# Second attention branch's scores: two products of 128 rows and two of 64 rows per head instead of four of 128

## The chip, the cores and the metric

The kernel runs on one core of one Trainium2 chip. The metric is the device time of one execution in microseconds, the median of the runs shown. TensorE (PE) multiplies; VectorE (DVE), ScalarE (ACT) and GpSimd (POOL) do the elementwise work; the SyncE queue (SP) issues most DMAs. "PEld" is the loading of a product's stationary operand into TensorE's array.

## The reference: what is computed

One layer of a diffusion backbone: 1024 latent tokens of width 1024 and 256 context tokens. The hidden states are modulated, projected to queries, keys, values and gates, and go through two attention branches of 8 heads of 64 with 2 key heads each. Branch A is windowed, with a sink; branch B, the second, is global: every token attends to all 1024 latent and all 256 context keys.

```python
def _gqa_scores(q, k):
    return jnp.einsum("bqhgd,bkhd->bhgqk", q, k).astype(jnp.float32) * (HEAD_DIM ** -0.5)
...
def _global_attention(q, k_all, v_all):
    def one_block(i):
        q_blk = lax.dynamic_slice_in_dim(q, i * BLOCK, BLOCK, axis=1)
        p = jax.nn.softmax(_gqa_scores(q_blk, k_all), axis=-1)
        return _gqa_values(p, v_all)
```

Then gates, an output projection, a residual LayerNorm, a convolutional feed-forward of width 2816 and a second LayerNorm.

## The kernel before

**Numbers in two parts.** Every float32 operand of a product is split into a high part, rounded to the format that TensorE takes, and a low part, the remainder. A general product is three passes (mm3, lines 375 to 378): high by high, high by low, low by high. For the scores the contraction is only 64 long, so both parts fit into the 128 rows of the array together.

**The scores before.** Per head, `q1` is the transposed query tile with the high part in rows 0 to 63 and the low part in rows 64 to 127, and `q2` the same with the halves swapped. The keys `KL` (1024 latent, one tile per key head) and `KC` (256 context) hold [high; low] in the same way. `qk` (line 757) makes two passes over all 128 rows: q1 by the keys gives high·high and low·low, q2 gives low·high and high·low. For branch B, `scores` (line 769) calls it for two banks of 512 keys, so four products of 128 rows by 512 columns per head; `cscores` (line 804) does the 256 context keys of a unit's four heads, eight products of 256 columns.

**Units.** The attention is cut into 32 units: 16 of branch A, then 16 of branch B, each with one tile of 128 queries and one key head, so four query heads. A unit's queries are split on POOL (`qsplit`), turned by four transposes on PE (`qturn`, line 736), copied out by ACT into `q1` (`qcopy`, line 741) and swapped into `q2` by two DMAs of 64 rows on SP (`qswap`, line 745, its two issues at lines 747 and 748). Then come the context scores (sx), the four heads' scores (s), the maximum on DVE (line 793), the exponential on ACT (line 802), transposes of the probabilities on PE (pt, line 847), their split into hi and lo on ACT, DVE and POOL, and the products with the values (av, line 856). Groups of the first output projection (ptb, lines 376 to 378) fill in between.

**The order.** In the attention stage all engines are under a manual schedule. `graph` (line 154) makes one entry per step with its engine, cost and a key; `plan` (line 86) is a list scheduler that takes on each engine the ready step with the smallest key. COST, KEY, FILL and SLACK are tables of numbers that only set this order; every engine then executes its list strictly in it. `qdm` is the step of the swap, `scx` that of the context scores, `sc1` that of one head's scores in branch B.

**The keys' preparation.** `kv_post` (line 667) runs ten times, for eight tiles of latent keys and two of context keys. Its last split (line 697) puts the high part of all four key heads (heads 0 and 1 of branch A, 2 and 3 of branch B) into columns 0 to 63 of `ks` and the low part into columns 64 to 127; transposes on PE turn them into rows, and ACT copies them to `KL` and `KC`.

Of the kernel before, what the change touches and what calls it, by code (L numbers as in the profile page):

```python
# [7 lines left out]
F32 = mybir.dt.float32  # L8
# [5 lines left out]
P = 128  # L14
# [4 lines left out]
NT = 8  # L19
HD = 64  # L20
# [19 lines left out]
PWB = 5  # L40
DAH = 3
SINK = 640
POOLED, FILL, SUMS = ((0,), (1, 6)), (16.988136, 27.931), ('ot1', 'ot1')
LOOK, SLACK = 24, (0, 0, 0, 0, 0)
D3AT = (7, 5), (7, 9), (4, 1), (4, 4), (4, 7), (4, 10), (5, 2)
NXS = 5
RAWB = 3
# [18 lines left out]
PE, ACT, DVE, POOL, SP = range(5)  # L66
# [19 lines left out]
def plan(ops, rings, free, look, slack):  # L86
# [5 lines left out]
    while any(todo):  # L92
# [25 lines left out]
        for b in o.uses:  # L118
# [6 lines left out]


COST = dict(
    qhi=(POOL, .38, .49), qlo=(POOL, .71, .825), qtr=(PE, .28, .55), qcp=(ACT, .47, .675), qdm=(SP, 1.1, 2.9),
    sc0=(PE, .70, .945), sc1=(PE, .91, 1.16), scx=(PE, .94, 1.19),
    pm0=(DVE, .80, .97), pm1=(DVE, 1.26, 1.43), pmx=(DVE, .40, .56),  # L130
    ex0=(ACT, .83, .98), ex1=(ACT, 1.14, 1.30), exx=(ACT, .49, .65),
    nr0=(DVE, .18, .28), nr1=(DVE, .34, .44), st=(PE, .11, .36), rc=(ACT, .20, .34), dn=(SP, .30, 2.2),
# [1 line left out]
    tr=(PE, .436, .685), hi=(ACT, .47, .675), lo=(DVE, .605, .765), cp=(ACT, .47, .675), ph=(POOL, .59, .70),  # L134
# [9 lines left out]
PRING = "pt", "s", "av"  # L144
RINGS = dict(pt=3, s=2, av=1, qs=1, q1=2, q2=2, p=8, hi=4, lo=4, ptr=2, up=1, ot=1, rb=2, wraw=1, wh=1, wl=1)

KEY = {'qh': -0.919337, 'qt': -1.197497, 'sc': -0.139853, 'scs': (0.199825, 0.270357),
           'scx': -3.142963, 'tr': 0.868828, 'tru': (0.216182, 0.070723),
           'av': 1.348883, 'st': 1.265771, 'out': 0.885708, 'exd': 1.273589, 'st1': 1.664154, 'wb': (27.969376, 29.459582),
           'wg': (31.81419, 33.291489, 33.170198, 33.528645), 'ge': -0.046198, 'gr': 4.26668}  # L150
UNITS = 32


def graph(x, key=KEY, pooled=((3,), (2, 6)), fill=None, ot=("ot0", "ot1")):
    ops, last = [], {}
    def op(kind, k, fn, after=(), takes=(), uses=()):
        e, occ, lat = COST[kind]
        o = Op(e, kind, occ, lat, k, fn, after, takes, uses, kind in PORT)
        ops.append(o)
        return o  # L160
# [10 lines left out]
    for hf in (0, 1):  # L171
# [6 lines left out]
        for c in range(4):  # L178
            r = op("gr", key["gr"] + .6 * (4 * hf + c), lambda hf=hf, c=c: x.gr(hf, c), [e], uses=[tile])
        op("gd", key["gr"] + .6 * (4 * hf + c), lambda hf=hf: x.gd(hf), [r], uses=[tile])  # L180
    units = []
    for u in range(UNITS):
        br, i, g = u // 16, u % 16 // 2, u % 2
# [7 lines left out]
        U = float(u)  # L191
        q1, q2 = Buf("q1"), Buf("q2")
        if u >= 2:
            qs, pt = Buf("qs"), Buf("pt")
            a = op("qhi", U + key["qh"], lambda u=u, b=qs: x.qhi(u, b), takes=[qs])
            b_ = op("qlo", U + key["qh"], lambda u=u, b=qs: x.qlo(u, b), [a], uses=[qs])
            qlo = b_
            c = op("qtr", U + key["qt"], lambda u=u, b=qs, p=pt: x.qtr(u, b, p), [b_], [pt], [qs])
            chain("qtr", c)
            d = op("qcp", U + key["qt"], lambda u=u, q=q1, p=pt: x.qcp(u, q, p), [c], [q1], [pt])  # L200
            qr = op("qdm", U + key["qt"], lambda u=u, q=q1, r=q2: x.qdm(u, q, r), [d], [q2], [q1])
        else:
            qlo, qr = None, op("qdm", U - 9, lambda: None, takes=[q1, q2])
            qr.occ = qr.lat = 0.0
# [4 lines left out]
        if br:  # L209
            s, pc = Buf("s"), Buf("p")  # L210
# [8 lines left out]
        for h in range(4):  # L219
            k = U + key["sc"] + key["scs"][br] * h  # L220
            s = Buf("pt" if nar and h < 2 else "s")
# [31 lines left out]
        t = op("st", kn, lambda u=u, p=pt: x.st(u, p), [n_], [pt])  # L253
        r = op("rc", kn, lambda u=u, p=pt, b=rb: x.rc(u, p, b), [t], [rb], [pt])
# [3 lines left out]
        av = Buf("av")  # L258
        avo, trs = [], []
        for j, n in enumerate(kt):  # L260
            k = U + key["tr"] + j * key["tru"][br]
            ka = U + key["av"] + j * key["tru"][br]
            pt, hi, lo = Buf("pt"), Buf("hi"), Buf("lo")
# [6 lines left out]
            if j in pooled[br]:  # L270
                rw = Buf("ptr")
                c = op("cp", k, lambda u=u, n=n, p=pt, r=rw: x.cp(u, n, p, r), [o], [rw], [pt])
# [19 lines left out]
        c = op(ot[br], ko - .4, lambda u=u, o=o_: x.ot(u, o), [b_], [o_], [rw, up])  # L292
# [8 lines left out]
    for f2 in range(4):  # L301
# [4 lines left out]
        c = op("wl", k - .9, lambda f2=f2, r=raw, l=wl: x.wl(f2, r, l), [b_], [wl], [raw])  # L306
# [15 lines left out]
    for f2 in (0, 1):  # L322
# [4 lines left out]
        c = op("wl", k + .1, lambda f2=f2, r=raw: x.wl(4 + f2, r, None), [b_], uses=[raw])  # L327
# [26 lines left out]
def layer_kernel(  # L354
# [6 lines left out]
    nc = tc.nc  # L361
# [4 lines left out]
    def split(src, hi, lo, hi_eng, lo_eng):  # L366
        if hi_eng is nc.scalar:
            cast[:] = [nc.scalar.copy(hi, src).ins]  # L368
        elif hi_eng is nc.gpsimd:
            nc.gpsimd.tensor_scalar(out=hi, in0=src, scalar1=1.0, scalar2=0.0, op0=ALU.mult, op1=ALU.add)  # L370
        else:
            hi_eng.tensor_copy(hi, src)
        low[:] = [lo_eng.tensor_tensor(out=lo, in0=src, in1=hi.bitcast(F32), op=ALU.subtract).ins]  # L373
# [88 lines left out]
    sc, scc = ht("sc"), ht("scc")  # L462
# [21 lines left out]
    st1 = {}  # L484
# [38 lines left out]
    for n in (0, 1):  # L523
        s = slice(n * HALF, (n + 1) * HALF)
# [11 lines left out]
    for k in range(KT):  # L536
# [5 lines left out]
        for t in range(NT):  # L542
            s = slice(t * P, (t + 1) * P)
# [114 lines left out]
    KL, KC, VT = [], [], []  # L658
# [8 lines left out]
    def kv_post(t, acc):  # L667
        st = {}

        def s1():  # L670
            kv = st["kv"] = ph1.tile([P, 512], F32, tag="kv", name=f"kv{t}", bufs=KVB)
            nc.vector.tensor_tensor(out=kv, in0=acc, in1=bias_kv, op=ALU.add)
            kb = st["kb"] = kv[:, 128:256].rearrange("p (h d) -> p h d", d=HD)
            vt = VT[t // 2][:, t % 2]
            v3 = kv[:, 256:512].rearrange("p (h d) -> p h d", d=HD)
            nc.scalar.copy(vt[:, :, 0:HD], v3)
            tp = pw(f"ktp{t}")
            st["tp"] = tp = [tp[:, n * P:(n + 1) * P] for n in range(4)]
            st["ss"] = rms_scale(kb, 2, f"k{t}", tp[3])
            if t < NT:  # L680
                st["tb"] = ph1.tile([P, 2, HD], F32, tag="tb", name=f"tbk{t}", bufs=4)
                gfold(st["tb"], 1, t, nc.vector)
                rope(nc.vector, kv[:, 0:128], kv[:, 0:128], 2, ropec[:, t], ropes[:, t], f"ka{t}", tp[0], tp[1])
            nc.gpsimd.tensor_tensor(out=vt[:, :, HD:P], in0=v3, in1=vt[:, :, 0:HD].bitcast(F32), op=ALU.subtract)

        def s2():
            kv, kb = st["kv"], st["kb"]
            rms_apply(kb, 2, st["ss"])
            tp = st["tp"]
            if t < NT:  # L690
                tb = st["tb"]
                rope(nc.vector, kv[:, 128:256], kv[:, 128:256], 2, tb[:, 0], tb[:, 1], f"kb{t}", tp[2], tp[3])
            else:
                nc.gpsimd.tensor_tensor(out=kb, in0=kb, in1=bc(gcol[:, 1], 2), op=ALU.mult)
            st["ks"] = ks = pw(f"ks{t}", (P, 4, P), R32)
            k3 = kv[:, 0:256].rearrange("p (h d) -> p h d", d=HD)
            split(k3, ks[:, :, 0:HD], ks[:, :, HD:P], nc.vector, nc.vector)

        def s3():
            ks = st["ks"]  # L700
            tr = acc_tile(f"ktr{t}", R32).rearrange("p (h q) -> p h q", h=4)
            for h in range(4):
                nc.tensor.transpose(tr[:, h], ks[:, h], identr)
            if t < NT:
                for h in range(4):
                    nc.scalar.copy(KL[h][:, t * P:(t + 1) * P], tr[:, h])
            else:
                nc.scalar.copy(KC[0][:, :, (t - NT) * P:(t - NT + 1) * P], tr)
        return [s1] + [lambda: None] * GAP + [s2, s3]

    class Unit:
# [33 lines left out]
        def qswap(self, slot):  # L745
            self.q2 = qp.tile([P, 512], R32, tag=f"q2{slot}", name=f"q2{self.id}", bufs=1)
            nc.sync.dma_start(self.q2[0:HD].bitcast(F32), self.q1[HD:P].bitcast(F32))
            nc.sync.dma_start(self.q2[HD:P].bitcast(F32), self.q1[0:HD].bitcast(F32))

        def qprep(self, mk, slot):  # L750
            self.qsplit(False)
# [17 lines left out]
        def scores(self, h, s):  # L769
            kh = self.br * 2 + self.g  # L770
            if self.br:
                for c in (0, 512):
                    self.qk(s[:, c:c + 512], h, KL[kh][:, c:c + 512])
                self.sv[h] = s
                return
            w, e = self.w, 512 if s.shape[1] == T else 256
            l = s[:, e - w:e]
            self.qk(l, h, KL[kh][:, self.k0:self.k0 + w], False)
            if w == 384:
                nc.tensor.matmul(l.rearrange("p (a b) -> p a b", b=P)[:, 0::2, :], identr, maskr, start=False, stop=True)  # L780
            elif self.i == 0:
                nc.tensor.matmul(l[:, 128:256], identr, maskr[:, 1], start=False, stop=True)
            else:
                nc.tensor.matmul(l[:, 0:128], identr, maskr[:, 0], start=False, stop=True)
            self.qk(s[:, e:e + NC], h, KC[0][:, kh])
            self.sv[h] = s[:, e - w:e + NC]
# [101 lines left out]
    units = [Unit(br, i, g) for br in (0, 1) for i in range(NT) for g in range(2)]  # L888
# [119 lines left out]
    for n, (gi, k, a) in enumerate(steps):  # L1008
# [20 lines left out]
        c = ready.pop(("c", k), None)  # L1029
# [100 lines left out]
    class Issue:  # L1130
# [30 lines left out]
        def qdm(self, u, q, r):  # L1161
            assert q.slot is not None
            units[u].qswap(r.slot)

        def scx(self, u, s):
            units[u].cscores(at(s, f"x{units[u].id}"))
# [883 lines left out]
    s = LN2_S[-1]  # L2050
# [22 lines left out]
    r = LN2_S[1]  # L2073
# [158 lines left out]
```

## Time and profile before

| what | value |
|---|---|
| median of 3 runs | 1521.51 us (1520.75 to 1522.1) |
| the profiled execution's own time | 1522.45 us |
| its span in the trace | 1520.6 us |
| PE, DVE, ACT, POOL busy | 1507.5, 1154.0, 800.3, 784.7 us |
| second branch's scores, start to end of the stage | about 445 to 712 us |
| granted TensorE clock, mean | 0.998 |

All times are in microseconds from the span's start unless marked ns. A row of a timeline gives start, duration, engine, source line, operation, output and inputs by the program's names, then rows\*columns and shapes of the operation. Durations of products are modelled and overlap: how closely products follow one another is read from their starts. A row of the waits gives who waited for what, the total, how often, and the longest.

### The profile page before, as it was taken

How to read it: one execution, taken by the hardware profiler on the slowest of the kernel's cores; microseconds unless marked ns; L12 is line 12 of the kernel's file. 1: busy time of each engine (PE TensorE's matmuls, PEld its weight loads, DVE VectorE, ACT ScalarE, POOL GpSimd, SP SyncE). 2: the span in 40 equal slices, each digit the busy share in tenths (PEclk: the TensorE clock that was granted, in tenths of full speed). 3: DMA queues.
4: the chain of work that ended last, by engine and by line, in shares of the span. 5: the costliest groups of instructions: out<-in, count | busy, mean ns of one | idle time of the engine just before them, and what ended most of it. 6: DMA issues, size and time to landing. Idle time of an engine off the chain costs nothing.

```text
span 1520.6 us, 21967 instructions
## 1 busy us (share of the span) xinstructions
PE 1507.5 (99%) x7640; PEld 1267.1 (83%) x7640; DVE 1154.0 (76%) x1735; ACT 800.3 (53%) x1406; POOL 784.7 (52%) x743
## 2 busy tenths in 40 slices
PE   9999999999999999999999999999999999999997
PEld 7888888889988888888888998888888888888886
DVE  7588847629777777787675888988888888657897
ACT  6422223448987777788233564444444444435533
POOL 0375303428896666585533556666677774021053
PEclk9999999999999999999999999999999999999999
DMA  9767673312447654823460322333344446996723
GB/s 376 257 220 256 219 242 110 94 40 66 119 119 170 170 122 105 175 66 105 154 166 22 108 90 101 111 112 111 111 111 111 111 111 192 368 270 207 253 80 111
DMA packets 112161, 229.73 MB, mean 151 GB/s; under 512 B 13521, under 2 KB 27345, under 8 KB 111954
## 3 DMA queue, kind: packets, MB, share of 16 engines
q1 hardware_dynamic: 97040, 199.72, 40.0%
q0 software_dynamic: 10400, 20.19, 8.6%
q10 hardware_dynamic: 4610, 8.42, 1.5%
q8 instruction: 60, 0.98, 0.3%
q14 instruction: 51, 0.42, 0.1%
HBM read 177.09 MB, written 65.87 MB: 160 GB/s over the span
## 4 chain that ended last, share of the span: by engine, by line
PE 44%; DVE 4%; issue 1%; DMA 1%; ACT 1%; POOL 0%; DVEq 0%; SPq 0%; ACTq 0%
PE p L377 3%; PE p L378 3%; PE p L376 3%; PE c L376 2%; PE a L376 2%; PE d L376 2%; PE a L378 2%; PE d L378 2%; PE c L378 2%; PE d L377 2%; PE c L377 2%; PE a L377 2%; PE y L378 2%; PE y L376 2%; PE y L377 2%; PE u L376 1%
## 5 line engine op out<-in xcount | busy, mean ns | idle before, releaser
L1234 DVE TENSOR_TENSOR lo<-pt,hi 128x512 fp32r<-128x512 f32 x188 | 126.8, 686 | 44.4 <-ACT hi L1228 35.0
L373 DVE TENSOR_TENSOR ld<-rd,hd 128x1024 fp32r<-128x1024 f32 x77 | 97.6, 1284 | 49.1 <-ACT hd L368 47.0
L1228 ACT CAST hi<-pt 128x512 fp32r<-128x512 f32 x188 | 108.4, 582 | 41.8 <-PE pt L847 23.5
L368 ACT CAST hd<-rd 128x1024 fp32r<-128x1024 f32 x77 | 79.5, 1050 | 86.5 <-PE p L378 53.0
L856 PE MATMUL av<-hi,VT 128*128 128x512 f32 x236 | 104.3, 443 | 0.2 <-POOL hi L1223 0.2
L377 PE MATMUL p<-ld,hd 128*128 128x512 f32 x264 | 102.8, 389 | 0.5 <-DVE ld L373 0.5
L376 PE MATMUL p<-hd 128*128 128x512 f32 x264 | 103.2, 391 | 0.0
L378 PE MATMUL p<-hd,ld 128*128 128x512 f32 x264 | 102.8, 389 | 0.0
L376 PE MATMUL g<-hh,whg 128*128 128x512 f32 x256 | 99.9, 390 | 0.0
L377 PE MATMUL g<-hl,whg 128*128 128x512 f32 x256 | 99.6, 389 | 0.0
L378 PE MATMUL g<-hh,wlg 128*128 128x512 f32 x256 | 99.6, 389 | 0.0
L856 PE MATMUL av<-lo,VT 128*128 128x512 f32 x236 | 99.3, 422 | 0.1
L373 POOL TENSOR_TENSOR wlg<-wg,whg 128x512 fp32r<-128x512 f32 x32 | 45.1, 1415 | 101.1 <-ACT whg L368 89.4
L793 DVE TENSOR_SCALAR_CACHE_REDUCE p<-s,cvt,nmc 128x1024 f32<-128x1024 f32 x64 | 85.6, 1339 | 11.0 <-PE s L760 7.1
L847 PEld LDWEIGHTS pt<-ident,p 128*128 128x128 f32 x512 | 63.6, 140 | 17.6 <-ACT rb L829 0.4
L802 ACT ACTIVATE p<-p,nm 128x1024 f32<-128x1024 f32 x64 | 73.9, 1155 | 7.0 <-DVE p L793 6.5
L847 PE MATMUL pt<-ident,p 128*128 128x128 f32 x512 | 76.6, 272 | 0.1
L759 PE MATMUL s<-KL,q 128*128 128x512 f32 (+2 forms) x186 | 72.9, 392 | 0.0
L793 DVE TENSOR_SCALAR_CACHE_REDUCE pa<-s,negsink 128x640 f32<-128x640 f32 (+1 forms) x58 | 49.3, 853 | 29.2 <-PE s L760 28.7
L368 ACT CAST wS<-s 128x512 fp32r<-128x512 f32 x76 | 45.3, 621 | 48.5 <-POOL s L1564 47.7
L760 PE MATMUL s<-KL,q 128*128 128x512 f32 (+2 forms) x186 | 69.5, 374 | 0.0
L368 ACT CAST wA<-ru 128x512 fp32r<-128x512 f32 x57 | 35.5, 623 | 63.0 <-PE d L378 34.8
(438 smaller groups left out, 5044.0 us busy)
## 6 DMA issues: line engine op xcount, KB each, us to landing
wml<-in_wmodT_dram SPq DMA_DIRECT2D x48, 512.0 KB
ru<-in_w_up_dram SPq DMA_DIRECT2D x38, 512.0 KB
rd<-td SPq DMA_DIRECT2D x55, 256.0 KB
rd<-sd SPq DMA_DIRECT2D x44, 256.0 KB
rd<-in_w_dn_dram SPq DMA_DIRECT2D x33, 256.0 KB
wm<-in_wmodT_dram SPq DMA_DIRECT2D x16, 512.0 KB
wg<-in_w_g_dram SPq DMA_DIRECT2D x32, 256.0 KB
q<-q SPq DMA_DIRECT2D x64, 128.0 KB
```

Source lines behind the costliest of these rows:

```text
L368: cast[:] = [nc.scalar.copy(hi, src).ins]
L373: low[:] = [lo_eng.tensor_tensor(out=lo, in0=src, in1=hi.bitcast(F32), op=ALU.subtract).ins]
L376: nc.tensor.matmul(ps, a[0], b[0], start=start, stop=False, skip_group_check=resumed)
L377: nc.tensor.matmul(ps, a[0], b[1], start=False, stop=False, skip_group_check=resumed)
L378: return nc.tensor.matmul(ps, a[1], b[0], start=False, stop=stop, skip_group_check=resumed).ins
L759: nc.tensor.matmul(o, self.q1[:, hs], ks, start=True, stop=False)
L793: nc.vector.tensor_scalar(out=p if self.br else p[:, self.pad + 1:SINK + 1], in0=self.sv[h], scalar1=self.scale()[:, hs] if self.br else - ...
L802: nc.scalar.activation(o, i, AF.Exp, bias=self.nm[:, hs], scale=-1.0, accum_out=acc)
L847: nc.tensor.transpose(tr[:, h * P:(h + 1) * P], src, ident)
L856: nc.tensor.matmul(self.av, v, self.parts[n][low], start=first, stop=self.left == 0)
L1228: nc.scalar.copy(hi, units[u].parts[n])
L1234: e.tensor_tensor(out=lo, in0=src, in1=hi.bitcast(F32), op=ALU.subtract)
```

## The change

In branch B a head's scores become two products of 128 rows and two of 64. `q1` is doubled by one more DMA, so that it holds [high; high]; `q2` becomes [low; low]. The key tiles 4 to 7 (keys 512 to 1023, the second bank) of heads 2 and 3 are stored turned, [low; high]; tiles 0 to 3 stay [high; low]. Then q1 by the keys gives high·high and high·low in one pass on either bank, whichever half is where. What remains is low·high: on bank 0 the high keys lie in rows 0 to 63, on bank 1 in rows 64 to 127, so two products of 64 rows each use a half of the array and a bank of their own. The term low·low is no longer computed for these keys. `cscores` keeps its eight products; with the new q1 and q2 they add up to the same four terms.

The diff, without the changed values of FILL, SLACK and KEY, which move the order (SLACK now lets ACT take a step up to 0.041673 later than the first ready one):

```diff
-    sc0=(PE, .70, .945), sc1=(PE, .91, 1.16), scx=(PE, .94, 1.19),
+    sc0=(PE, .70, .945), sc1=(PE, .80, 1.05), scx=(PE, .94, 1.19),
...
+            if br:
+                qr = op("qd2", U + key["qt"] + key.get("qd", .3), lambda u=u: x.qd2(u), [qr], uses=[q1, q2])
...
-            split(k3, ks[:, :, 0:HD], ks[:, :, HD:P], nc.vector, nc.vector)
+            turned = 2 if NT // 2 <= t < NT else 4
+            split(k3[:, 0:turned], ks[:, 0:turned, 0:HD], ks[:, 0:turned, HD:P], nc.vector, nc.vector)
+            if turned < 4:
+                split(k3[:, turned:4], ks[:, turned:4, HD:P], ks[:, turned:4, 0:HD], nc.vector, nc.vector)
...
-            nc.sync.dma_start(self.q2[HD:P].bitcast(F32), self.q1[0:HD].bitcast(F32))
+            hi = slice(HD, P) if self.br else slice(0, HD)
+            nc.sync.dma_start(self.q2[HD:P].bitcast(F32), self.q1[hi].bitcast(F32))
+
+        def qdouble(self):
+            nc.sync.dma_start(self.q1[HD:P].bitcast(F32), self.q1[0:HD].bitcast(F32))
...
             if self.br:
+                hs = slice(h * P, (h + 1) * P)
                 for c in (0, 512):
-                    self.qk(s[:, c:c + 512], h, KL[kh][:, c:c + 512])
+                    nc.tensor.matmul(s[:, c:c + 512], self.q1[:, hs], KL[kh][:, c:c + 512], start=True, stop=False)
+                for c, r in ((0, slice(0, HD)), (512, slice(HD, P))):
+                    nc.tensor.matmul(s[:, c:c + 512], self.q2[r, hs], KL[kh][r, c:c + 512], start=False, stop=True)
                 self.sv[h] = s
                 return
```

Two places show what moves in the engines' lists. On PE, a head of the unit of query tile 3, key head 0 in branch B (s is the scores' tile in PSUM, KL the keys, the two q are q1 and q2; the output's shape stands behind). Before:

```order
L759 MATMUL s_3_0_1_6303<-KL_2114,q_3_0_6026 128x512
L760 MATMUL s_3_0_1_6303<-KL_2114,q_3_0_6040 128x512
L759 MATMUL s_3_0_1_6303<-KL_2114,q_3_0_6026 128x512
L760 MATMUL s_3_0_1_6303<-KL_2114,q_3_0_6040 128x512
L847 MATMUL pt_2_1_3_6319<-ident,p_2_1_0_6046 128x128
```

And of the change:

```order
L783 MATMUL s_3_0_1_6326<-KL_2114,q_3_0_6040 128x512 x2
L785 MATMUL s_3_0_1_6326<-KL_2114,q_3_0_6049 128x512 x2
L836 MATMUL pts_2_1_6337<-ident,sm_2_1_6001 4x128
L859 MATMUL pt_2_1_3_6339<-ident,p_2_1_0_6062 128x128
L859 MATMUL pt_2_1_3_6339<-ident,p_2_1_1_6116 128x128
```

The products are still four (two rows of two); the first two now use q1, the last two a half each of q2.

On SP, the first unit of branch B (its q is q_0_0; q_7_1 and rb_6_1 belong to the last units of branch A, dn is the row of denominators on its way through DRAM, rb its return). Before:

```order
L833 DMA dn_6_1_4765<-rb_6_1_4756 4x128
L837 DMA rb_6_1_4756<-dn_6_1_4765 64x2x128 x2
L747 DMA q_0_0_4830<-q_0_0_4822 64x512
L748 DMA q_0_0_4830<-q_0_0_4822 64x512
L833 DMA dn_7_0_4891<-rb_7_0_4882 4x128
```

And of the change:

```order
L845 DMA dn_6_1_4792<-rb_6_1_4783 4x128
L752 DMA q_0_0_4820<-q_0_0_4807 64x512
L754 DMA q_0_0_4820<-q_0_0_4807 64x512
L849 DMA rb_6_1_4783<-dn_6_1_4792 64x2x128 x2
L757 DMA q_0_0_4807<-q_0_0_4807 64x512
```

The swap moved ahead of a return, and the doubling (line 757) stands behind that return. It writes what the swap reads, so it waits for the swap to land, and what follows on SP waits with it.

On PE, between the transposes of this unit's queries and its first context product (sx) stand 42 instructions before and 49 now: three products with the values (av) and four transposes (pt) more. On DVE the split in `kv_post` was one cast and one subtraction over four heads for each tile; in tiles 4 to 7 it is two of each over two heads.

More of the change, by code (lines that the diff above doesn't have):

```diff
@@ L42 @@
 SINK = 640
-POOLED, FILL, SUMS = ((0,), (1, 6)), (16.988136, 27.931), ('ot1', 'ot1')
-LOOK, SLACK = 24, (0, 0, 0, 0, 0)
+POOLED, FILL, SUMS = ((0,), (1, 6)), (16.967521, 28.322416), ('ot1', 'ot1')
+LOOK, SLACK = 24, (0, 0.041673, 0, 0, 0)
 D3AT = (7, 5), (7, 9), (4, 1), (4, 4), (4, 7), (4, 10), (5, 2)
@@ L127 @@
 COST = dict(
-    qhi=(POOL, .38, .49), qlo=(POOL, .71, .825), qtr=(PE, .28, .55), qcp=(ACT, .47, .675), qdm=(SP, 1.1, 2.9),
-    sc0=(PE, .70, .945), sc1=(PE, .91, 1.16), scx=(PE, .94, 1.19),
+    qhi=(POOL, .38, .49), qlo=(POOL, .71, .825), qtr=(PE, .28, .55), qcp=(ACT, .47, .675), qdm=(SP, 1.1, 2.9), qd2=(SP, .55, 2.6),
+    sc0=(PE, .70, .945), sc1=(PE, .80, 1.05), scx=(PE, .94, 1.19),
     pm0=(DVE, .80, .97), pm1=(DVE, 1.26, 1.43), pmx=(DVE, .40, .56),
@@ L145 @@
 RINGS = dict(pt=3, s=2, av=1, qs=1, q1=2, q2=2, p=8, hi=4, lo=4, ptr=2, up=1, ot=1, rb=2, wraw=1, wh=1, wl=1)
[L147 to L150, printed above, removed]
+KEY = {'qh': -1.103714, 'qt': -1.25896, 'sc': -0.140191, 'scs': (0.199825, 0.274707),
+           'scx': -2.422445, 'tr': 0.837184, 'tru': (0.216182, 0.070723),
+           'av': 1.353407, 'st': 1.272243, 'out': 0.598234, 'exd': 0.738635, 'st1': 1.586911, 'wb': (27.945695, 29.067685),
+           'wg': (31.866029, 33.59625, 33.392372, 33.775142), 'ge': -0.351061, 'gr': 4.607115}
 UNITS = 32
@@ L1163, in qdm, with qd2 @@
             units[u].qswap(r.slot)
+        def qd2(self, u):
+            units[u].qdouble()
         def scx(self, u, s):
```

## The prediction

> **What bounds the kernel now.** I read the page first. Its first part gives each engine's busy time, share of the span and instruction count; the first line of its part on the chain says where that chain runs.
>
> ```profile
> span 1520.6 us, 21967 instructions
> PE 1507.5 (99%) x7640; PEld 1267.1 (83%) x7640; DVE 1154.0 (76%) x1735; ACT 800.3 (53%) x1406; POOL 784.7 (52%) x743
> ```
>
> TensorE is busy in 99% of the span. The average hides stages, so I asked next for the stretch from 445 to 712 us, which holds every score of the second branch: length, then busy time of PE, PEld, DVE, ACT and POOL, the granted clock, DMA share and GB/s. Of the same stretch I read what PE and its weight loads waited for (total, times, longest).
>
> ```profile
> 445.00:712.00 267.00, 266.78 (x1584) 223.53 (x1584) 203.80 (x428) 207.92 (x457) 175.19 (x216) 1.00 0.56 134
> ```
>
> ```profile
> PEld av L856 <- POOL hi L1223: 0.6, 1, 0.6
> PEld av L856 <- POOL lo L1234: 0.4, 1, 0.4
> PE av L856 <- POOL hi L1223: 0.2, 1, 0.2
> PEld av L856 <- issue: 0.2, 1, 0.2
> ```
>
> So this stage is a list of TensorE instructions worked off one after another: 266.8 of 267 us busy at full clock, 1.4 us of waits. DVE has 63 us to spare and ACT 59. Time taken off TensorE here comes off the kernel, until another engine has no time left.
>
> A busy PE says nothing of how closely its instructions follow each other. The timeline does: start, duration, instruction. First the products of one head, then the weight loads (PEld) of the same microsecond.
>
> ```profile
> 567.01 0.40 PE L856 MATMUL av<-lo,VT 128*128 128x512 f32 x1
> 567.25 0.39 PE L759 MATMUL s<-KL,q 128*128 128x512 f32 x1
> 567.48 0.39 PE L760 MATMUL s<-KL,q 128*128 128x512 f32 x1
> 567.70 0.39 PE L759 MATMUL s<-KL,q 128*128 128x512 f32 x1
> 567.93 0.39 PE L760 MATMUL s<-KL,q 128*128 128x512 f32 x1
> 568.16 0.60 PE L847 MATMUL pt<-ident,p 128*128 128x128 f32 x4
> ```
>
> ```profile
> 560.65 0.19 PEld L856 LDWEIGHTS av<-hi,VT 128*128 128x128 f32 x1
> 560.76 0.19 PEld L856 LDWEIGHTS av<-lo,VT 128*128 128x128 f32 x1
> ...
> 567.01 0.19 PEld L759 LDWEIGHTS s<-KL,q 128*128 128x128 f32 x1
> 567.25 0.19 PEld L760 LDWEIGHTS s<-KL,q 128*128 128x128 f32 x1
> 567.48 0.19 PEld L759 LDWEIGHTS s<-KL,q 128*128 128x128 f32 x1
> 567.71 0.19 PEld L760 LDWEIGHTS s<-KL,q 128*128 128x128 f32 x1
> ```
>
> Three readings carry the forecast. **Step:** the four products of a head take 568.16 - 567.25 = 0.91 us, 0.23 each, although one shows a duration of 0.39: the next starts while the last 0.16 us of the one before are still in the array. **Load:** two loads with nothing between them start 0.11 apart (560.65, 560.76). **One ahead:** each load starts when the product *before* its own starts (the load for the product at 567.48 starts at 567.25). Loads run one product ahead, not two.
>
> **The change, part by part.**
>
> *The products (scores).* There are 128 + 128 of them, 64 heads of four, as the groups by line say (count, busy us, mean ns, then the idle time before):
>
> ```profile
> L759 PE MATMUL s<-KL,q 128*128 128x512 f32 x128 | 52.7, 411 | 0.0
> L760 PE MATMUL s<-KL,q 128*128 128x512 f32 x128 | 50.5, 395 | 0.0
> ```
>
> The changed kernel has as many: two of 128 rows, then two of 64 rows on different halves of the array and different banks. No instruction disappears; the gain is all in what the last two share. No product of 64 rows is in the trace, so I bound the pair. From below: both stream at once, 0.23 in place of 0.46, which saves 64 x 0.23 = 14.6 us. From above: they follow each other and each change between full and half rows costs something, for which the largest number in these rows is the 0.16 that a product still spends in the array plus a bare load of 0.11, at two changes a head: 2 x 0.27 = 0.54 lost, less the 0.12 derived next, 0.42 x 64 = +27 us.
>
> The value I take follows from the three readings. The first half product's load is hidden under the second full product. The second half's load starts when the first half starts, so the second half starts 0.11 later and streams 0.23; the next instruction's load fits under it. The pair takes 0.34, the head 2 x 0.23 + 0.34 = 0.80, **0.117 less than 0.91** (3 x 0.2275 + 0.11 = 0.79): 64 x 0.117 = 7.5 us. It is the value that needs no behaviour which these rows don't already show, save that two halves stream at once.
>
> *Changes of kind.* For a price of going from one kind of work to another and back the nearest rows are transposes followed by products:
>
> ```profile
> 560.33 0.60 PE L847 MATMUL pt<-ident,p 128*128 128x128 f32 x4
> 560.68 0.48 PE L856 MATMUL av<-hi,VT 128*128 128x512 f32 x1
> 561.00 0.40 PE L856 MATMUL av<-lo,VT 128*128 128x512 f32 x1
> 561.24 0.60 PE L847 MATMUL pt<-ident,p 128*128 128x128 f32 x4
> ```
>
> Four transposes at the load's 0.11 and two products at 0.23 make 0.90; the rows take 0.91. So there and back costs 0.01, and I put 64 x 0.01 = 0.6 us on the change. These are full-row instructions on both sides, so this is a neighbour's price.
>
> The Trainium skill speaks against the change here: "TensorEngine Tiling (Array Packing)", Key Properties, says that changing the tiling mode, unlike changing the tile, drains the engine. By it the sum would be that of the rival that ends slower; no run here shows a half-row product, so nothing yet confirms or denies it.
>
> *The doubling DMA (qd2) and SP.* Each second-branch unit gets a third transfer of the swaps' size, issued once the swaps have landed, since it overwrites what they read; 16 in all, 2 MB against 134 GB/s over 267 us, which is small. Only its latency can hurt, and only where TensorE reaches the unit's first product (sx) early. That is the first unit. Before, in timelines of PE, ACT and the queue of SP:
>
> ```profile
> 439.94 0.46 PE L738 MATMUL pt<-identr,qs 128*128 128x128 f32 x4
> ...
> 445.65 0.36 PE L759 MATMUL sx<-KC,q 128*128 128x256 f32 x1
> ```
>
> ```profile
> 440.81 0.57 ACT L743 CAST q<-pt 128x512 fp32r<-128x512 f32 x1
> ```
>
> ```profile
> 437.37 0.24 SPq L833 DMA_DIRECT2D dn<-rb  x1
> 438.57 1.29 SPq L837 DMA_DIRECT2D rb<-dn  x2
> ...
> 441.41 0.50 SPq L747 DMA_DIRECT2D q<-q  x1
> 441.95 1.05 SPq L748 DMA_DIRECT2D q<-q  x1
> ```
>
> From transposes to the swaps' last issue: 3.1 us. A landing takes over 0.96 (dn issued by 437.61, its reader issued at 438.57) and under 2.65 (443.00 to sx at 445.65). Twice that, and an issue of 0.5, puts the doubled queries 5.5 to 8.9 us after the transposes. The new order has the 5.7 us of PE work between them, three products (0.69) and four transposes (0.44) more: 6.8. So the wait is 0 to 2.1 us, and I take 0.3. SP holds the next rb and dn transfers behind the doubling's wait, a landing at most, against units some 17 us long. Later units stand wider apart; of the last one before, these rows:
>
> ```profile
> 685.10 0.45 PE L738 MATMUL pt<-identr,qs 128*128 128x128 f32 x4
> ...
> 697.31 0.36 PE L759 MATMUL sx<-KC,q 128*128 128x256 f32 x1
> ```
>
> 12.2 us, over the 8.9 of the slowest case, so I count no wait for them.
>
> *The key tiles (kv_post).* Four tiles split their heads in two pairs: two more casts and two more subtractions each. The groups of the tile ks, with min/median/max ns, and the stage they stand in:
>
> ```profile
> L372 DVE CAST ks<-kv x10: 277/288/1369, 251.1 to 303.3; 128x256 fp32r<-128x256 f32 x10
> L373 DVE TENSOR_TENSOR ks<-kv,ks x10: 406/412/1396, 251.4 to 304.7; 128x256 fp32r<-128x256 f32 x10
> ```
>
> ```profile
> 240.00:280.00 40.00, 40.00 (x194) 33.22 (x193) 30.28 (x108) 18.81 (x52) 11.64 (x15) 1.00 0.39 113
> ```
>
> At full price, though half as wide, that is at most 4 x 0.70 = 2.8 us of DVE, at least nothing, beside a PE that is busy in 40.00 of 40 us with DVE 10 us idle. I count zero; if the cover were gone it would be up to 2.8.
>
> *The re-planned order.* The weights move every attention unit's instructions a little. TensorE's list is otherwise the same, and it waited 1.4 us in this stage, so a better order can give at most that. A worse one shows up as waits on DVE or ACT; with 260 us left for the stage DVE would stand at 78% and ACT at 80%. I take zero, within -1.4 and, as an estimate from as much again, +1.4.
>
> **Sum.** -7.5 + 0.6 + 0.3 = -6.6. The profiled run took 1522.45 us with its span of 1520.6, so 1515.9 for it; it stands 0.9 above the median of the runs shown, 1521.51, from which the same sum gives **1514.9**.
>
> **Rivals.**
>
> *The array empties at each change of rows (slower).* Place: before the first half product and after the second. Price: the 0.16 that a product still spends in the array, twice a head, 0.32 less 0.117 is +0.20, times 64 is +13.0 and 0.3 for the first unit: 1534.8; with loads that can't run ahead, +27: 1549. It decides from 0.06 us a change on, where the gain is eaten. For it: full and half rows are different uses of the array, and nothing in the trace changes between them. Against it: transposes and products change places at 0.01.
>
> *Both halves stream at once from the start.* If loads for different halves don't wait for one another, the pair takes 0.23: -14.6 + 0.6 + 0.3, 1507.8. For it: the halves share neither rows nor banks. Against it: loads in these rows always run one product ahead.
> The Trainium skill's "TensorE: Matmul & The Clock Gate", Part 3, has this case: products on different row groups start about 4 ns apart. By that figure the sum would be this rival's; the rows here, with one load ahead, don't show it.
>
> *No sharing.* The change doesn't do what it says: half products follow one another like full ones, 0.23 each. Then only the small debits remain, +0.9: 1522.4, within what counts as the same (a measurement of this kernel tells apart about 0.2%, 3 us).
>
> *The freed time meets another wait* (late doublings, a worse order, each unit some 0.4 us late): the gain is eaten to about zero, 1521.
>
> **How the numbers follow.** Forecast 0.52, streaming at once 0.15, no sharing 0.06, other waits 0.06, emptying 0.21. Faster is the forecast with the second, and a hundredth of the waits: 0.68. Same: 0.11, the third and the rest of the fourth. Slower: 0.21. The range starts below the second case by the 1.4 of the order, 1506, and ends at 1525, which takes in no sharing, other waits and an emptying of up to 0.085 a change; it leaves the rest of the emptying out, under 2 in 10. The forecast's own range is 1512 to 1518.
>
> **What would show it.** In the changed trace a head's four score products should start 0.23, 0.23 and 0.11 apart and the next instruction 0.23 after the last: 0.80 in all. 0.69 means streaming at once; 0.91, no sharing; over 1.0, or a gap ahead of the first half or after the second, emptying. sx of the first unit should start within a microsecond of its place in the order, DVE and ACT of the stage should stay near 80%, and no new wait of PE should total more than 2 us. Wrong it would be above all by the pair's time, which no row here shows.

## The result, and the profile after

The changed kernel takes 1532.3 us (median of 4 runs, 1530.56 to 1534.32) against 1521.25 of the kernel before: 11 us slower, ratio 1.0073 with a 95% interval of 1.0055 to 1.009. The profiled execution has a span of 1531.3, 10.7 over the one before.

```profile
span 1531.3 us, 22035 instructions
...
PE 1517.2 (99%) x7640; PEld 1252.9 (82%) x7640; DVE 1151.4 (75%) x1743; ACT 802.1 (52%) x1406; POOL 783.5 (51%) x743
```

TensorE executes as many products as before (7640) and is busy 9.7 us longer. DVE, ACT and POOL are busy as long as before, so none of them has become the bound. The timeline of PE says where the time went. Of one head in the changed kernel, from the first product of 128 rows on:

```profile
562.75 0.63 PE L783 MATMUL s<-KL,q 128*128 128x512 f32 x2
563.30 0.49 PE L785 MATMUL s<-KL,q 64*128 64x512 f32 x2
563.73 0.66 PE L859 MATMUL pt<-ident,p 128*128 128x128 f32 x4
564.14 0.48 PE L868 MATMUL av<-lo,VT 128*128 128x512 f32 x1
564.46 0.39 PE L868 MATMUL av<-hi,VT 128*128 128x512 f32 x1
564.69 0.60 PE L859 MATMUL pt<-ident,p 128*128 128x128 f32 x4
565.04 0.48 PE L868 MATMUL av<-lo,VT 128*128 128x512 f32 x1
```

Two things stand in these rows. The two half-row products share a row of 0.49 us, and one of them alone has 0.49 (the durations below): they start together and stream side by side, as the change meant. But the row for two full products lasts from 562.75 to 563.30, 0.55 in place of twice 0.23, the halves hold the array for 0.43, and the transposes behind them take 0.41 (563.73 to 564.14) where others take 0.35 (564.69 to 565.04). Together that is 1.39 from the first product to the end of the transposes; with four full products it is 0.91 + 0.35 = 1.26.

The loads show what happens in between, here with the time that PEld sat idle ahead of them in brackets, and the tile q gives the durations (min/median/max ns).

```profile
562.52 0.42 PEld L783 LDWEIGHTS s<-KL,q 128*128 128x128 f32 x2
563.30 0.19 PEld L785 LDWEIGHTS s<-KL,q 64*128 64x128 f32 x2 [0.36 <-issue]
563.73 0.42 PEld L859 LDWEIGHTS pt<-ident,p 128*128 128x128 f32 x4 [0.24 <-DVE p L805]
```

```profile
L783 PE MATMUL s<-KL,q x128: 387/397/482, 449.4 to 722.0; 128*128 128x512 f32 x128
...
L785 PE MATMUL s<-KL,q x128: 491/493/502, 449.9 to 722.4; 64*128 64x512 f32 x128
```

Before, each load started when the product ahead of its own started, and was hidden under it. The halves' loads start only at 563.30, with the halves themselves: for the 0.36 us ahead of them, while the second full product runs, nothing is loaded, and nothing for 0.24 us ahead of the transposes' loads, while the halves run. So each half product carries its load (0.49 in place of 0.39), and both changes of rows are spent waiting. The last row puts its 0.24 down to DVE, but in the waits of PEld over the whole kernel 40 of these stand with as much and no releaser. The halves' own loads stand there 64 times, once for each head:

```profile
PEld s L785 <- issue: 23.4, 64, 0.4
PEld pt L859 <- issue: 9.7, 40, 0.2
```

The third finding is in the waits of PE, which had no such row before:

```profile
PE sx L768 <- DMA q<-q: 2.9, 2, 2.4
```

Twice the first products of a unit waited for the doubled queries, 0.4 us in the first unit, where I had looked, and 2.4 in the third. The queue of SP shows that unit's swap, its doubling and, in its waits from 455 to 476 us, the time between them (two waits, the longest 9.0):

```profile
461.84 0.50 SPq L752 DMA_DIRECT2D q<-q  x1
462.39 0.59 SPq L754 DMA_DIRECT2D q<-q  x1
472.02 0.46 SPq L757 DMA_DIRECT2D q<-q  x1
```

```profile
SPq L757 <- DMA q<-q: 10.2, 2, 9.0
```

The swap took 9.0 us to land, beside DMA engines that were full: from 460 to 470 us, the first row of the next fence, their mean share was 1.04. The fence behind it lists, of the issues from 461 to 473 us, a transfer of 1 MB by POOL that took 15.4 us to land. Of the 16 doublings in this trace eleven were issued 1.8 to 3.1 us behind their swap, one 6.6 with other issues of SP between, and four 5.4 to 9.0 us behind it: the four whose swap ran beside a transfer of this kind. The second row has the price that came after: in the ten microseconds around the pause the granted clock is 0.83. The clock's records have one stretch of 3.4 us at half speed there, 1.7 us lost, on top of the 2.4.

```profile
460.00:470.00 10.00, 10.00 (x65) 7.46 (x64) 7.72 (x19) 7.29 (x17) 7.33 (x11) 1.00 1.04 173
470.00:480.00 10.00, 7.57 (x37) 5.98 (x36) 6.48 (x14) 6.07 (x16) 3.53 (x5) 0.83 0.85 227
```

```profile
sd<-in_w_dn_dram POOLq DMA_DIRECT2D x1, 1024.0 KB, 15.4
```

### The profile page after: what moved, and what is told of

Same layout as the page of the kernel before. It is cut to its first block, busy times and chain, and to the rows that moved or that the text cites. A ratio compares the mean times of both kernels' runs of the same rounds, so it can differ in the third digit from the quotient of the medians.

```text
span 1531.3 us, 22035 instructions
## 1 busy us (share of the span) xinstructions
PE 1517.2 (99%) x7640; PEld 1252.9 (82%) x7640; DVE 1151.4 (75%) x1743; ACT 802.1 (52%) x1406; POOL 783.5 (51%) x743
## 4 chain that ended last, share of the span: by engine, by line
PE 96%; DVE 2%; DMA 1%; issue 0%; ACT 0%; POOL 0%; SPq 0%; DVEq 0%; ACTq 0%
PE av L868 7%; PE pt L859 7%; PE g L378 4%; PE g L380 4%; PE g L379 4%; PE p L378 4%; PE p L379 4%; PE p L380 4%; PE d L380 2%; PE a L380 2%; PE c L380 2%; PE d L378 2%; PE c L378 2%; PE a L378 2%; PE c L379 2%; PE d L379 2%
## 5 line engine op out<-in xcount | busy, mean ns | idle before, releaser
L859 PEld LDWEIGHTS pt<-ident,p 128*128 128x128 f32 x512 | 60.4, 140 | 21.4 <-issue 7.0
L1249 POOL TENSOR_TENSOR lo<-ptr,hi 128x512 fp32r<-128x512 f32 x48 | 62.1, 1294 | 3.6
L1238 POOL TENSOR_SCALAR hi<-ptr 128x512 fp32r<-128x512 f32 x48 | 29.9, 623 | 66.4 <-ACT ptr L1233 63.7
```

The lines of the kernel that those rows point to most:

```text
L859: nc.tensor.transpose(tr[:, h * P:(h + 1) * P], src, ident)
L1238: nc.gpsimd.tensor_scalar(out=hi, in0=units[u].parts[n], scalar1=1.0, scalar2=0.0, op0=ALU.mult, op1=ALU.add)
L1249: e.tensor_tensor(out=lo, in0=src, in1=hi.bitcast(F32), op=ALU.subtract)
```

## The experiments

**Theory A:** the array empties at each change between full and half rows, so that no load is hidden there. (By the modelled durations above the full products end at 563.38 and the halves at 563.79; the loads behind them come 0.08 and 0.06 us earlier, so "empties" is meant to within that.) It costs each head more than the shared streaming brings, some 0.11 us net. The late doublings add a few microseconds. **Theory B, the rival:** the changes of rows are nearly free, and the late doublings and the new order make up the loss. A second rival to A is that every pair of half-row products is slow in itself, whatever stands around it.

### Full rows in the changed kernel (e1_full_rows)

```diff
-    nc.tensor.matmul(s[:, c:c + 512], self.q2[r, hs], KL[kh][r, c:c + 512], start=False, stop=True)
+    nc.tensor.matmul(s[:, c:c + 512], self.q2[:, hs], KL[kh][:, c:c + 512], start=False, stop=True)
```

> The changed kernel with its two products of 64 rows replaced by two of 128 rows of the same q2 ([low; low] by the whole key tile, so low by low is computed as well); order, doubling and turned keys stay. Theory A (the array empties at each change of rows, 0.11 us a head net): 64 x 0.11 = 7 us faster than the changed kernel, about 1525, still 4 us over before for the late doublings; a head takes 0.92 us again. Theory B (the late doublings and the new order cost it all, row changes are nearly free): no faster than the changed kernel, 1532, or slower by the lost side-by-side streaming.

Measured: 1525.69 us (10 runs), ratio to before 1.0036 (1.0022 to 1.0049), 6.6 under the changed kernel. A gives 7, B nothing. A head takes 0.92 us again in the trace (572.73 to 573.65). Its runs spread from 1523.9 to 1533.1, and its profiled execution, 1531.3 long, is among its longest; it shows why: late doublings, 7.3 us of waits in two places.

```profile
PE sx L768 <- DMA q<-q: 7.3, 2, 4.5
```

That a doubling lands at another time in each run is what I take this spread to mean; only one execution was traced. So I compare medians here and take the doublings out of the way in the later experiments.

### No doubling (e2_no_doubling)

```diff
         def qdouble(self):
-            nc.sync.dma_start(self.q1[HD:P].bitcast(F32), self.q1[0:HD].bitcast(F32))
+            pass
```

> The changed kernel without the doubling DMA: q1 keeps [high; low], so high by low of the second branch's scores is replaced by low by low or left mixed. Theory A: only the wait of 2.9 us and the stretch at half clock behind it (3.4 us at half, 1.7 lost) go, 4.6 us: about 1527.7, and the heads still take 1.0 us. Theory B: all of the loss goes, 1521 or less.

Measured: 1528.97 us (4 runs), ratio 1.0049 (1.0034 to 1.0064): 3.3 under the changed kernel and still 7.5 over before. The waits of PE have no row for the queries. B is wrong: most of the loss stays. A had expected 4.6, which was the price in one execution.

### Every pair twice (e3_pairs_twice)

```diff
+    for n in (0, 1):
         for c, r in ((0, slice(0, HD)), (512, slice(HD, P))):
-            nc.tensor.matmul(..., start=False, stop=True)
+            nc.tensor.matmul(..., start=False, stop=n == 1)
```

> The changed kernel with every pair of 64-row products issued twice in a row (low by high is added twice). Theory A (the change of rows costs, the pair itself streams at once): the second pair adds one stream of 0.23 us a head, 64 x 0.23 = 14.7, about 1547. Rival (every 64-row pair takes the 0.43 us that it shows now): 64 x 0.43 = 27, about 1560.

Measured: 1544.36 us (4 runs), ratio 1.0158 (1.014 to 1.0175), 12.1 over the changed kernel and 14.4 over f1_two_copies below. That one has no late doublings, and this one's profile has next to none (0.6 us), so it is the closer neighbour. So a second pair costs the stream that A gives it, and the rival, 27, falls. A head in its timeline of PE:

```profile
564.69 0.63 PE L783 MATMUL s<-KL,q 128*128 128x512 f32 x2
565.25 0.73 PE L786 MATMUL s<-KL,q 64*128 64x512 f32 x4
565.92 0.65 PE L860 MATMUL pt<-ident,p 128*128 128x128 f32 x4
```

One pair held the array for 0.43, two hold it for 0.67 (565.25 to 565.92): the second adds 0.24. It is the change that costs, not the pair.

### Both halves on the same rows (e4_same_half)

```diff
-    for c, r in ((0, slice(0, HD)), (512, slice(HD, P))):
+    for c, r in ((0, slice(0, HD)), (512, slice(0, HD))):
```

> The changed kernel with both 64-row products on rows 0 to 63 (the second bank's low by high becomes low by low). If the halves stream together because they stand on different rows, they now follow each other: 0.23 us a head more, 14.7 us, about 1547. If different banks are enough, no change: 1532.

Measured: 1543.99 us (4 runs), ratio 1.0151 (1.0136 to 1.0166), 11.7 over the changed kernel, 14.1 over f1_two_copies. On the same rows they follow each other, although their banks differ: the pair holds the array for 0.66 us (563.31 to 563.97) where it held it for 0.43.

```profile
563.31 0.73 PE L785 MATMUL s<-KL,q 64*128 64x512 f32 x2
563.97 0.27 PE L836 MATMUL pts<-ident,sm 128*4 128x128 f32 x1
```

```profile
563.31 0.29 PEld L785 LDWEIGHTS s<-KL,q 64*128 64x128 f32 x2 [0.36 <-issue]
565.32 0.29 PEld L785 LDWEIGHTS s<-KL,q 64*128 64x128 f32 x2 [0.37 <-issue]
```

Their two loads take 0.29 one after the other, where loads on different halves shared 0.19. So what the change was meant to bring is real: one stream a head, 14 us in all.

### The chain of transfers taken out (f1_two_copies, f5_full_two_copies)

In f1_two_copies ACT makes two copies, and the DMAs depend on one copy each; f5_full_two_copies has the edit of e1_full_rows as well.

```diff
-            nc.scalar.copy(self.q1, self.qtr)
+            nc.scalar.copy(self.q1[0:HD], self.qtr[0:HD])
+            nc.scalar.copy(self.q2[HD:P], self.qtr[HD:P])
...
+                nc.sync.dma_start(self.q1[HD:P].bitcast(F32), self.q1[0:HD].bitcast(F32))
+                nc.sync.dma_start(self.q2[0:HD].bitcast(F32), self.q2[HD:P].bitcast(F32))
```

> The changed kernel without the chain of transfers: in the second branch ACT copies the high half of the turned queries into q1 and the low half into q2 in two copies, and two DMAs that don't wait for each other fill the other halves. The half-row products stay. Theory A: no PE wait on the queries' DMA and no stretch at half clock, a head still takes 1.0 us: what leaving the doubling out gave, 3 to 4 us under the changed kernel, 1528 to 1529, still 7 us over before. Theory B (doubling and order are all of it): 1521 or less.

> The same, with four products of 128 rows per head (low by low is computed as well): what is left of the change is the order, the turned keys and the two copies. Theory A: the row changes' 7 us are gone too, 1521.5, no more than 1.4 either side of before. If the new order itself costs, it stays above 1523.

Measured: f1_two_copies 1529.92 us (5 runs), ratio 1.0053 (1.004 to 1.0066); f5_full_two_copies 1522.85 us (12 runs), ratio 1.0008 (0.9999 to 1.0017). Neither waits for the queries. f1_two_copies is 0.9 above what A gave. The two differ in nothing but 64-row against 128-row products, with the same operands and order of banks, and the difference is **7.1 us** where A gave 7. Their runs don't overlap (1529.0 to 1530.6 against 1519.3 to 1526.9), and the traces agree: from a head's first product to the start of what follows, the 64 heads take 64.5 us against 60.8, and what follows takes some 0.06 more each, together some 7 us. What is left of the change in f5_full_two_copies, 1.3 us over before, can't be told from nothing and lies within the 1.4 expected; its profile has one wait that before had not (f1_two_copies has it too, with 1.7 us):

```profile
PE av L873 <- POOL lo L1251: 2.7, 1, 2.7
```

A head of it, with the four full products back to back, is as before: 0.92 us.

```profile
569.70 0.62 PE L788 MATMUL s<-KL,q 128*128 128x512 f32 x2
570.15 0.63 PE L790 MATMUL s<-KL,q 128*128 128x512 f32 x2
570.62 0.60 PE L864 MATMUL pt<-ident,p 128*128 128x128 f32 x4
```

### Two heads per change (f2_two_heads, f3_two_heads_order)

On top of f1_two_copies, one step of the plan computes two heads: four full products, then both pairs. It takes both score tiles at once, and KEY, FILL and SLACK were searched anew for it; f3_two_heads_order differs in these and in which tiles POOL splits.

```diff
+                for n in (0, 1):
+                    hs = slice((h + n) * P, (h + n + 1) * P)
+                    for c in (0, 512):
+                        nc.tensor.matmul(s[n][:, c:c + 512], self.q1[:, hs], ..., start=True, stop=False)
+                for n in (0, 1):
...
+                        nc.tensor.matmul(s[n][:, c:c + 512], self.q2[r, hs], ..., start=False, stop=True)
```

> As f1_two_copies, but two heads are computed together: four products of 128 rows, then two pairs of 64, so one change there and back for two heads, in an order searched anew for it, which keeps TensorE waiting more often since it needs both score tiles free. Theory A: two heads take about 1.74 us in place of 2.0 (4 x 0.23, 0.09 to change, 0.34 and 0.32 for the pairs, 0.06 behind them); without the added waits that would be 8 us under f1_two_copies, 1520 to 1521, and with them more, by what PE is seen to wait. Rival (every pair pays, not every change): 2.0 us for two heads.

> As f2_two_heads with another order, in which TensorE should find its operands ready more often. Theory A: two heads take about 1.7 us as in f2_two_heads, where they took 1.68; the time is that of f2_two_heads, 1527.9, less the waits that the order takes away, at best some 7 us, so 1521 to 1528: the pairing alone can bring the kernel back to about before, and under it only if next to no waits are left.

Measured: f2_two_heads 1527.86 us (4 runs), ratio 1.0048 (1.0033 to 1.0063). Two heads of it:

```profile
577.97 1.09 PE L793 MATMUL s<-KL,q 128*128 128x512 f32 x4
578.99 0.73 PE L797 MATMUL s<-KL,q 64*128 64x512 f32 x4
579.65 0.66 PE L871 MATMUL pt<-ident,p 128*128 128x128 f32 x4
580.07 0.48 PE L880 MATMUL av<-lo,VT 128*128 128x512 f32 x1
```

1.68 us, or 1.74 with the 0.06 of the transposes behind: A's number, against 2.1 for two single heads with theirs and 1.84 for two of before. This pair is the shortest of the 32; in the mean a pair takes 1.80 with the 0.06, and two heads of f5_full_two_copies take 1.90, so that the gain is 0.10 either way. So the price belongs to the change and is halved by halving the changes, and the rival falls. The kernel's time shows only 2.1 of the 8 us against f1_two_copies, and with runs from 1526.6 to 1533.8 even that is not clear. The new order has more waits of PE for DVE and POOL, but how much of the 8 us they took I can't separate, since the whole order differs.

f3_two_heads_order measured 1537.14 us (4 runs), ratio 1.0099 (1.0082 to 1.0115), outside what was expected: its order has fewer but longer waits, and with each of the two longest goes a stretch of 6.8 us at half clock in the clock's records, 3.4 lost each.

```profile
PE av L880 <- POOL lo L1263: 3.1, 1, 3.1
PE b L382 <- POOL O L897: 3.0, 1, 3.0
```

No version was found that beats the kernel before. Whether heads in pairs would, in an order without these waits, stays open: 32 x 0.10 is 3.2 us at most.

## Why the prediction was wrong

It was wrong in sign: 1514.9 was forecast, and 1532.3 lies outside the range; of the rivals the emptying one, given 0.21, has the mechanism that the runs show.

- **What bounds the kernel** was read rightly: a list of TensorE instructions, in which each change of their time comes through. It also meant that the loss came through.
- **The pair (-7.5).** The reading "one load ahead" did not carry over. Loads for different halves run side by side, the halves start together, and sharing saves a whole stream, 14 us (e4_same_half), twice what I took; here the rival given 0.15 was right. By the Trainium skill's "TensorE: Matmul & The Clock Gate", Part 3, such products start about 4 ns apart. These rows agree with it: the row of two lasts 0.49 and one lasts 0.49, and the trace has 3 to 4 ns between the two starts of every pair.
- **Changes of kind (+0.6): the step that failed.** I priced the changes "there and back costs 0.01" after transposes and products, which use full rows alike. Measured: a head with its bare load behind takes 1.04 us (0.55 + 0.43 + 0.06), and with the sharing and free changes it would take 3 x 0.23 = 0.69. There and back costs **0.35 us, 22 us in all**, thirty-five times the price taken, which turns -14 into a loss of some 8 (f1_two_copies less f5_full_two_copies measures +7.1). The Trainium skill's "TensorEngine Tiling (Array Packing)", Key Properties, has the rule that a change of tiling mode drains the engine. These rows agree with it, as far as their durations go; my neighbour's price set it aside on evidence that held no such change.
- **The emptying rival** had the place right and a price near the measured one, 0.32 there and back, but a saving of half the size: 0.32 less 0.117 is +0.20 a head, 13 us, where 0.35 less 0.23 is +0.12. That its 1534.8 stands near the measured time is luck, since the doublings and the rest added 3.7 us that it did not have. The bound from above, +27, was added up wrongly: a pair that follows one another has no 0.117 to take off, and 64 x 0.54 is 35. My top of the range allowed 0.085 a change beside a small saving; the real change costs 0.17 on average.
- **The doubling (+0.3).** The first unit waited 0.4 us, as taken. "I count no wait" for the others failed. The bound of a landing came from the first unit alone, under 2.65 us, and the third unit's swap took 9.0 beside the 1 MB transfers. Before, the same swap had 9.6 us until its sx (462.35 to 471.95) and PE did not wait, so two landings in a row lost the slack that one had. The trace of before could have warned: in the stretch 461 to 473 us it has the same 1 MB transfer, 17.6 us to landing (the first fence below). Price: 2.4 (changed kernel less f1_two_copies) to 3.3 us (less e2_no_doubling).
- **The key tiles (0)** held: PE stays busy in 40.00 of the 40 us from 240 on and DVE goes from 30.28 to 30.39.
- **The re-planned order (0)** held within what can be measured: f5_full_two_copies is at 1.0008 (0.9999 to 1.0017). Of the "1.4 us of waits" that a better order could have won, 1.2 were waits of the weight loads and only 0.2 of PE itself.

```profile
sd<-in_w_dn_dram POOLq DMA_DIRECT2D x1, 1024.0 KB, 17.6
```

```profile
240.00:280.00 40.00, 40.00 (x195) 33.21 (x194) 30.39 (x110) 18.80 (x52) 11.60 (x15) 1.00 0.38 113
```

The loss of 11 us is thus 7.1 for the changes of rows net of the sharing, 2.4 for the doublings and 1.3 for the rest. These are steps from one median to the next, so that they add up by construction; each rests on its own pair of kernels alone, and the last is not clear of nothing.

## What to carry to other kernels

Half-row products on different halves ran side by side here, but the kernel paid for each switch between full and half rows: 0.35 us there and back, more than the 0.23 of one stream of 512 columns. Put as many half-row products behind one switch as the accumulators allow: one pair lost, two pairs won 0.10 us in the products themselves, though not yet in the time of a whole kernel. And price a mode that the trace doesn't show by a bound, not by the nearest habit of other instructions. A transfer that must wait for another should be given the landing time of the busiest stretch, not of a quiet one.

## What was not expected of the hardware

A pause of TensorE could cost more than its length. In the changed kernel, after 2.4 us of waiting, the granted clock stood at half for 3.4 us (1.7 lost); in e1_full_rows it did so for 3.4 us behind a pause of 2.8 and for 6.8 us with one of 4.5, and in f3_two_heads_order for 6.8 us with each of its pauses of 3.1 and 3.0. Pauses of 1.7 (f1_two_copies) and 2.7 us (f5_full_two_copies) left no such stretch in the middle of the kernel, so length alone doesn't decide it in these traces; what does was not tested. The second of the two in f3_two_heads_order lies in this stretch, whose granted clock is 0.94, or 3.6 us lost in 60:

```profile
700.00:760.00 60.00, 56.90 (x291) 44.89 (x290) 35.06 (x59) 32.49 (x68) 40.31 (x44) 0.94 0.42 140
```
